# A two-layer generator backbone on one core: the framework's order of instructions made with a simulated time line

## The chip, the core and the metric

The kernel runs on one NeuronCore of a Trainium2 chip. Five engines work side by side, each through its own queue in order: TensorE (PE, matmuls and transposes, results in PSUM), VectorE (DVE), ScalarE (ACT), GpSimd (POOL) and SyncE (SP, which here issues DMAs). An instruction that needs another engine's result waits for a semaphore, and everything behind it in its queue waits too. The metric is the device time of one execution in microseconds, as the median of several runs.

## The reference

Two layers over 256 latent tokens, with 256 context tokens beside them in layer 0, model width 1024. Each layer is a token mixer and then a convolutional feed-forward network (FFN 2816 wide); each of the two is followed by a LayerNorm of a weighted sum. Layer 0 mixes by a bidirectional mLSTM (4 heads, inner width 2048), layer 1 by multi-head latent attention (8 heads). Shift, scale and gate of each sub-layer come from the condition vectors.

```python
ml = _modulation(c, ada_w[i], ada_b[i])            # six vectors: shift, scale, gate, twice
hl = _modulate(x, ml[0], ml[1])
yl, yc = mixer(hl, hc, ...)                        # mLSTM in layer 0, MLA in layer 1
x = _layer_norm(ALPHA * x + ml[2] * yl, ln_g[i, 0], ln_b[i, 0])
f = _conv_ffn(_modulate(x, ml[3], ml[4]), ffn_w_in[i], ffn_conv_w[i], ffn_conv_b[i], ffn_w_out[i])
x = _layer_norm(ALPHA * x + ml[5] * f, ln_g[i, 1], ln_b[i, 1])
```

In layer 0 the context goes through the same weights, with its own modulation. In layer 1 it only gives keys and values.

## The kernel before

**Products.** Every float32 product is three matmuls of split operands, in `mm3`: hi·hi (L383), hi·lo (L384) and lo·hi (L385), where hi is the operand rounded to TensorE's fast float32 form and lo is the rest. So every weight block of 128 x 1024 needs three steps before use: a DMA into `raw`, a cast on ScalarE (L323) that gives hi, and a subtraction on VectorE (L326) that gives lo. The class `Stream` does this in the order of use, up to eight blocks ahead (`AHEAD`), with three ordinary split buffers (`w`, `NB`) and some wide ones (`wu`). In the same way activations are split by `split` (L388 the cast, L389 the subtraction).

**Stages, in order of time.** `start_up` (first modulation and the first five `up` products), `w_up`, `w_og`, `w_v` (up to about 400 us), `w_qk` with the heads of the mLSTM, then the output product "mout", once for the context (`pc`) and once for the latent tokens (`pl`), the FFN of layer 0 (`ffn_pre`, `ffn_in`, then `w_fout0` with the products y21, y22 and yt4), the keys and values of layer 1 (`mla_ctx`, `mla_kv`, tiles dkv, kn and v), `mla`, the output product "aout", the FFN of layer 1 and its output product "fout1" with the last LayerNorm.

**Work beside the products.** Much of the VectorE and ScalarE work is in Python generators, which the product loops advance a step at a time (`tick`, `drain`): `head` (mLSTM weights W, lines 1008 to 1037: exponentials, multiplication with the scores, normalisation at L1023 and L1025, transposes PT at L1037), `post` (normalisation of a head's output `oh` at L1107, transposes `hnT` at L1113, result `hn`), `ln_rows` (gate L1141, residual L1142, statistics L1144, normalisation L1172 and L1173), `ln_T` (transposes `zT` at L1199, modulation `zm`, split into `h0`, `hc`, `hl` or `h1` at L1211 and L1212), `ln_x` (L1227, L1228), and in `w_fout0` the residual (gate L1441, addition L1442). A second list, `bg2`, spreads the modulation vectors of the later sub-layers over the products: one gate sum `junk` on VectorE (L512) per row block, let go by a small ScalarE copy (`gate`, L527).

**Product tails.** `outmm` multiplies one weight block with all banks of the output before the next block. For the last blocks (`TAIL`: 4 in mout, 7 in aout, 6 in fout1) it holds the weights and writes the loops the other way round, bank by bank, so that the first banks are finished early:

```python
            for t in range(2):
                for ps, cs in pss[t]:
                    for k, w in zip(tail, ws):
                        mms(k, w, t, ps, cs)
```

**What sets the order.** The program text is not the order of each engine's queue. The framework (`tile.TileContext`) tracks the dependencies between tiles, gives out buffers and semaphores, and lets its scheduler choose the order in which the instructions are put in the engines' queues. Two things bind it: `manual_schedule` around `start_up` keeps TensorE, VectorE and ScalarE in the written order there, and `keep_in_program_order` pins a few single instructions. Everything else is at the scheduler's choice.

## Time and profile before

| | |
|---|---|
| median of 3 runs | 1388.25 us (1387.74 to 1389.04) |
| profiled execution, its own time | 1389.13 us |
| its span in the profile | 1387.4 us, 19172 instructions |
| mean granted TensorE clock | 0.997 |
| TensorE matmuls busy | 1355.8 us (98 % of the span), 6903 |
| VectorE busy | 1075.0 us (77 %) |
| ScalarE busy | 699.2 us (50 %) |
| GpSimd busy | 121.2 us (9 %) |
| HBM | 262.90 MB read, 33.46 MB written, 214 GB/s over the span |

A row of the profile's groups has the line of the kernel, the engine, the operation, `out<-in` by tile names, the count, then the busy time and the mean time of one in ns, then the idle time of the engine ahead of them with what ended it. In the timeline a row has start, duration, engine, line and operation, and in brackets the idle time before it and what it waited for. PEld is TensorE's loading of the stationary operand, which overlaps the matmuls.

### The profile page before, as it was taken

The numbers are of one execution on the slowest core, as the hardware profiler recorded it, in microseconds if no ns is written. First come the engines' busy times: TensorE is split into PE (matmuls) and PEld (weight loads), VectorE is DVE, ScalarE is ACT, GpSimd is POOL, SyncE is SP. The second block draws the span as 40 slices with busy tenths as digits, with TensorE's granted clock in tenths as the row PEclk, the third lists the DMA queues.
The fourth block names the chain that finished last, engine by engine and source line by source line (L and its number), as shares of the span: only waits on it lengthen the run. The fifth ranks groups of instructions, "written<-read, shape, count | busy, mean of one in ns | idle before, by whom it ended". The sixth has DMA issues, their size and how long they took to land.

```text
span 1387.4 us, 19172 instructions
## 1 busy us (share of the span) xinstructions
PE 1355.8 (98%) x6903; PEld 1140.1 (82%) x6903; DVE 1075.0 (77%) x1726; ACT 699.2 (50%) x1179; POOL 121.2 (9%) x215
## 2 busy tenths in 40 slices
PE   7999999999999999999999999999999999999997
PEld 3788888888788888878798888888777898899986
DVE  6599757687688697788799878668898789777773
ACT  6585534435444545375643434334547567455560
POOL 0033000011011011120002000000001001000000
PEclk9999999999999999999999999999999999999999
DMA  9689847879666374766747877647987426367750
GB/s 339 217 292 325 289 152 248 237 261 326 210 205 203 104 231 140 242 196 223 242 143 242 295 234 234 211 148 234 310 224 224 137 99 207 116 188 230 209 183 31
DMA packets 97903, 297.63 MB, mean 215 GB/s; under 512 B 12136, under 2 KB 24808, under 8 KB 97808
## 3 DMA queue, kind: packets, MB, share of 16 engines
q1 hardware_dynamic: 68672, 218.52, 48.9%
q0 software_dynamic: 17472, 57.57, 13.4%
q10 hardware_dynamic: 11664, 20.32, 4.0%
q8 instruction: 54, 0.88, 0.3%
q14 instruction: 41, 0.34, 0.1%
HBM read 262.90 MB, written 33.46 MB: 214 GB/s over the span
## 4 chain that ended last, share of the span: by engine, by line
PE 86%; DVE 7%; DMA 3%; ACT 2%; issue 2%; ACTq 0%; SPq 0%; DVEq 0%
PE fin L383 9%; PE fin L384 9%; PE fin L385 9%; PE tok L383 6%; PE tok L385 6%; PE tok L384 6%; PE qk L383 4%; PE qk L384 4%; PE qk L385 4%; PE y L384 4%; PE y L385 4%; PE y L383 4%; PE up L383 2%; PE up L385 2%; PE up L384 2%
## 5 line engine op out<-in xcount | busy, mean ns | idle before, releaser
L326 DVE TENSOR_TENSOR w<-raw,w 128x1024 fp32r<-128x1024 f32 (+3 forms) x290 | 347.9, 1203 | 159.1 <-ACT w L323 158.3
L323 ACT CAST w<-raw 128x1024 fp32r<-128x1024 f32 (+3 forms) x290 | 300.3, 1037 | 331.6 <-PE fin L385 105.0
L384 PE MATMUL fin<-h,w 128*128 128x256 f32 (+1 forms) x696 | 231.7, 333 | 0.0
L385 PE MATMUL fin<-h,w 128*128 128x256 f32 (+1 forms) x696 | 231.4, 333 | 0.0
L383 PE MATMUL fin<-h,w 128*128 128x256 f32 (+1 forms) x696 | 231.2, 333 | 0.1
L512 DVE SCALAR_TENSOR_TENSOR junk<-ar,bc 128x1024 f32<-128x1024 f32 x128 | 155.9, 1218 | 4.9 <-ACT bc L554 2.3
L384 PEld LDWEIGHTS fin<-h,w 128*128 128x128 f32 x696 | 132.2, 190 | 13.0 <-DVE h L1212 0.2
L383 PEld LDWEIGHTS fin<-h,w 128*128 128x128 f32 x696 | 131.9, 190 | 13.2 <-ACT h L1211 0.3
L385 PEld LDWEIGHTS fin<-h,w 128*128 128x128 f32 x696 | 132.2, 190 | 12.7
L383 PE MATMUL qk<-xc,w 128*128 128x512 f32 x256 | 100.7, 393 | 0.0
L385 PE MATMUL qk<-xc,w 128*128 128x512 f32 x256 | 99.9, 390 | 0.0
L384 PE MATMUL qk<-xc,w 128*128 128x512 f32 x256 | 99.8, 390 | 0.0
L383 PEld LDWEIGHTS qk<-xc,w 128*128 128x128 f32 x256 | 48.1, 188 | 10.2 <-issue 0.4
L385 PEld LDWEIGHTS qk<-xc,w 128*128 128x128 f32 x256 | 48.1, 188 | 9.9
L384 PEld LDWEIGHTS qk<-xc,w 128*128 128x128 f32 x256 | 48.1, 188 | 9.6
L383 PE MATMUL up<-hT,w 128*128 128x512 f32 x128 | 50.5, 394 | 0.5 <-ACT hT L388 0.5
L384 PE MATMUL up<-hT,w 128*128 128x512 f32 x128 | 50.1, 392 | 0.4 <-DVE hT L389 0.4
L385 PE MATMUL up<-hT,w 128*128 128x512 f32 x128 | 50.1, 391 | 0.3 <-DVE w L389 0.3
L383 PE MATMUL tok<-w,hT 128*128 128x512 f32 x128 | 49.8, 389 | 0.0
L384 PE MATMUL tok<-w,hT 128*128 128x512 f32 x128 | 49.8, 389 | 0.0
L385 PE MATMUL tok<-w,hT 128*128 128x512 f32 x128 | 49.8, 389 | 0.0
L326 DVE TENSOR_TENSOR wu<-raw,wu 128x1024 fp32r<-128x1024 f32 (+1 forms) x33 | 39.1, 1200 | 8.2 <-ACT wu L323 7.9
(453 smaller groups left out, 3036.6 us busy)
## 6 DMA issues: line engine op xcount, KB each, us to landing
raw<-in_ws SPq DMA_DIRECT2D x287, 512.0 KB, 4.5
ar<-in_adaT SPq DMA_DIRECT2D x80, 512.0 KB, 4.7
adaw<-in_ada_w SPq DMA_DIRECT2D x32, 256.0 KB, 6.5
t2d<-raw ACTq DMA_DIRECT2D x13, 512.0 KB, 6.2
raw<-t2d SPq DMA_DIRECT2D x13, 512.0 KB, 6.3
raw<-in_ws POOLq DMA_DIRECT2D x13, 512.0 KB, 8.0
zr<-fd ACTq DMA_DIRECT2D x33, 128.0 KB, 3.2
xmd<-xr POOLq DMA_DIRECT2D x16, 256.0 KB, 5.4
```

Source lines behind the costliest of these rows:

```text
L323: k.nc.scalar.copy(h[:, :cols], src)
L326: k.nc.vector.tensor_sub(l[:, :cols], src, h[:, :cols])
L383: mm(out, w[0], x[0], start=start, stop=False)
L384: mm(out, w[0], x[1], start=False, stop=False)
L385: mm(out, w[1], x[0], start=False, stop=stop)
L512: nc.vector.scalar_tensor_tensor(o, w, 1.0, self.bc[j], op0=ALU.mult, op1=ALU.mult, accum_out=col[:, k, j:j + 1])
```

## The change

The one statement in `kernel` that opens the framework's context, at L1967, is given an option. With it the scheduler chooses its order along a simulated time line of the engines, instead of by its default rule. Kernel functions, buffers, constants and pins stay as they are.

```diff
-    with tile.TileContext(nc) as tc:
+    with tile.TileContext(nc, schedule_with_timeline_sim=True) as tc:
         build(tc, off, aps, out)
```

## The prediction

> **What bounds the kernel now.** I read the busy shares first, then the chain of work that ended last.

> ```profile
> PE 1355.8 (98%) x6903; PEld 1140.1 (82%) x6903; DVE 1075.0 (77%) x1726; ACT 699.2 (50%) x1179; POOL 121.2 (9%) x215
> PE 86%; DVE 7%; DMA 3%; ACT 2%; issue 2%; ACTq 0%; SPq 0%; DVEq 0%
> ```

> TensorE is busy for 1355.8 of 1387.4 us. The change leaves every instruction in place and alters only the order, so TensorE's own work is the same. All that can be won is its idle time, 31.6 us, and all that can be lost is new idle time. The second view is the busy time by stretch (the columns are stretch, its length, then PE, PEld, DVE, ACT and POOL busy with their counts, TensorE's granted clock, DMA share, GB/s).

> ```profile
> 0.00:100.00 100.00, 89.86 (x378) 62.04 (x379) 71.29 (x106) 66.72 (x108) 11.35 (x25) 1.00 0.82 281
> 100.00:600.00 500.00, 499.97 (x2261) 411.09 (x2260) 375.96 (x603) 236.53 (x406) 53.83 (x94) 1.00 0.70 225
> 600.00:700.00 100.00, 98.05 (x462) 80.33 (x461) 86.14 (x147) 59.92 (x105) 8.70 (x16) 1.00 0.74 234
> 700.00:1000.00 300.00, 299.91 (x1397) 251.11 (x1396) 243.91 (x369) 125.98 (x203) 21.64 (x40) 1.00 0.69 225
> 1000.00:1100.00 100.00, 91.51 (x472) 77.28 (x470) 89.82 (x169) 58.80 (x113) 9.72 (x14) 0.98 0.71 216
> 1100.00:1200.00 100.00, 96.95 (x627) 87.02 (x628) 86.35 (x162) 63.74 (x121) 6.20 (x12) 1.00 0.41 138
> ```

> Ten of the idle microseconds lie before 100 us (mostly the first loads) and 7.5 after 1300 us (the last LayerNorm, behind TensorE's last matmul). Between 100 and 600 us and between 700 and 1000 us there is nothing to win. That leaves 1.95 + 8.49 + 3.05 = 13.5 us in three stretches, the ones where VectorE is busy for 86 to 90 %. There TensorE and VectorE are both nearly full, and what counts is the order in which VectorE serves TensorE. The waits of TensorE (total us, times, longest) say who is late:

> ```profile
> PE adar L474 <- ACT adas L388: 6.7, 1, 6.7
> PE y L384 <- DVE w L326: 3.2, 3, 1.3
> PE y L383 <- ACT u L1421: 2.0, 1, 2.0
> PE zT L1199 <- DVE z L1172: 1.8, 1, 1.8
> PE dkv L383 <- ACT hl L1211: 1.5, 1, 1.5
> ```

> The first is the start, whose order on TensorE, VectorE and ScalarE is fixed by hand in both kernels. The other four are single events in the three stretches.

> **What the change does, part by part.** The built orders can be compared without times. The multiset of instructions is the same on every engine. The fewest instructions that must move to turn one order into the other are 587 of 6905 on TensorE, 417 of 1568 on VectorE, 201 of 1224 on ScalarE, 17 on GpSimd and 21 on SyncE. Three patterns hold most of them. (1) Where a weight's low half is awaited, TensorE now runs the hi·hi products (L383) of all open banks first. (2) The closing products of `outmm` (`last=True`), before done bank by bank, are interleaved over the banks. (3) On VectorE the weight subtractions L326 and the gate sums `junk` L512 are pulled ahead of head, residual and LayerNorm work, or, between 1004 and 1030 us, residual work is pulled ahead of L326. The prices of these movable pieces:

> ```profile
> L326 DVE TENSOR_TENSOR w<-raw,w 128x1024 fp32r<-128x1024 f32 (+3 forms) x290 | 347.9, 1203 | 159.1 <-ACT w L323 158.3
> L323 ACT CAST w<-raw 128x1024 fp32r<-128x1024 f32 (+3 forms) x290 | 300.3, 1037 | 331.6 <-PE fin L385 105.0
> L512 DVE SCALAR_TENSOR_TENSOR junk<-ar,bc 128x1024 f32<-128x1024 f32 x128 | 155.9, 1218 | 4.9 <-ACT bc L554 2.3
> ```

> *Zone A, 605 to 630 us (head 3 beside mout).* In before, VectorE finishes the attention weights W and TensorE transposes them at once:

> ```profile
> 607.53 0.50 PE L384 MATMUL y<-w,hn 128*128 128x512 f32 x1 [1.06 <-DVE w L326]
> 610.79 0.74 DVE L1025 SCALAR_TENSOR_TENSOR W<-W,R 128x512 f32<-128x512 f32 x1
> 611.73 0.82 PE L1037 MATMUL PT<-ident,W 128*128 128x128 f32 x6
> 614.67 1.67 DVE L1107 TENSOR_SCALAR oh<-oh,ss 128x512 f32<-128x512 f32 x4
> 620.70 0.39 PE L385 MATMUL y<-w,hn 128*128 128x512 f32 x1
> ```

> In the new order that last W operation stands 15 places later. Counted from 605.1 us, VectorE must first do six L326 and five junk sums (starts 1.14 us apart: 12.5 us), the four oh (1.6) and some 4.3 us of small work: 18.4 us, so W ends at 623.5 without any wait, and at about 625.7 if two of the pulled-ahead subtractions wait a cast of 1037 ns each. TensorE's transposes were pushed 37 places back, which gives cover: it does the mout products up to those that ended at 620.7 in before. It gains the 1.06 us wait and a smaller one, and so gets there at about 619.7. It stalls 3.8 to 6 us, then the chain transposes, split, next products adds about 1.5 us. I take the longer stall, since raw weights arrive just in time here (DMA share 0.74 in this stretch), so net +7.5; bounds +2.6 to +8.5.

> *Zone B, 690 to 708 us (mout tail, LayerNorm, ffn_pre).*

> ```profile
> 694.81 0.68 DVE L1141 TENSOR_TENSOR z<-y,gate 128x512 f32<-128x512 f32 x1
> 706.79 0.54 DVE L1172 TENSOR_SCALAR z<-z,mv,rs 128x512 f32<-128x512 f32 x1
> 707.90 1.80 PE L1199 MATMUL zT<-ident,z 128*128 128x128 f32 x15
> ```

> Before, the first bank is finished 8 us ahead of the last, and VectorE's twelve LayerNorm operations start at 694.8, beside the other banks. In the new order all four banks end within 1.6 us of the tail's end, and a junk sum stands ahead of the first L1141. VectorE then begins at 698.5, has 12 operations of 0.6 us and the small ones, and reaches the last L1172 at about 707.3 to 708.0. TensorE's cover (ffn_pre up to 707.9) is used up to the last 0.6 us already, so nearly all of that delay is paid: +1, bounds -0.8 (only the covered wait at 690.5) to +4.

> *Zone C, 1004 to 1085 us (FFN products y21, y22, yt4 and the key/value part of layer 1).*

> ```profile
> 1004.00 0.50 PE L383 MATMUL y<-w,fz 128*128 128x512 f32 x1 [2.04 <-ACT u L1421]
> 1020.52 1.21 DVE L326 TENSOR_TENSOR w<-raw,w 128x1024 fp32r<-128x1024 f32 x1
> 1023.26 0.39 PE L384 MATMUL y<-w,fz 128*128 128x512 f32 x1
> 1027.72 0.50 PE L384 MATMUL y<-w,fz 128*128 128x512 f32 x1 [1.35 <-DVE w L326]
> ```

> The residual operations L1441 and L1442 (0.6 us each) now stand ahead of the subtractions. The subtraction that ends at 1021.7 in before stands ten places later: from 1003.5 us VectorE has 5 full subtractions ahead of and with it and some 30 shorter operations, which ends at about 1027.5. TensorE wants that half at 1023.3, so it stalls there. After it the next one (1027.7 in before) is no longer the late one, so the net delay by 1030 us is 3 us, not 4.3. Later in the zone z_norm and the hc and hl copies stand 3 to 8 places back, behind weight subtractions and behind L1227/L1228; TensorE waits there already (1.5 us for hl), so such delays are paid in full: another +3, since several come in a row and part of each is hidden by the one before. Zone C +6, bounds +1 to +9.

> *Zone E, 1174 to 1192 us (aout tail, LayerNorm, first FFN products of layer 1).*

> ```profile
> 1174.00 0.39 PE L385 MATMUL y<-wu,oT 128*128 128x512 f32 x1
> 1175.54 0.68 DVE L1141 TENSOR_TENSOR z<-y,gate 128x512 f32<-128x512 f32 x1
> 1186.39 0.28 PE L385 MATMUL y<-wu,oT 128*128 128x256 f32 x1
> 1188.96 0.54 DVE L1172 TENSOR_SCALAR z<-z,mv,rs 128x512 f32<-128x512 f32 x1
> 1189.56 1.53 PE L1199 MATMUL zT<-ident,z 128*128 128x128 f32 x12 [1.84 <-DVE z L1172]
> ```

> Before, the first bank ends at 1174.0, 12.4 us ahead of the last, and only a bank of 256 columns is left for VectorE after 1186.4; the normalisation follows 2.6 us later. Interleaved, the first two banks end about 5.2 us ahead of the last. VectorE then has two L326 and the operations of all five banks to do, some 10.5 us of work from 1181.2 on, so the normalisation comes about 6 us after the last matmul. TensorE has nothing else to do there: +3.5, bounds +1.5 to +4.5.

> *The rest.* A head's normalisation at 1155 us stands behind one more subtraction: +0.5 (0 to +1). The low-half waits left over, 3.2 us less those already counted, and small ones go to pattern (1): -1 (-3 to 0). Between 100 and 600, 700 and 1000, and after 1200 us the swaps cost nothing, because TensorE is full and its operands are ready some microseconds ahead; if that cover failed, one swap costs one L326, 1.2 us. The 21 moved DMA issues on SyncE and the 17 on GpSimd shift by a few places in queues; I price them at nothing, bounded by one weight load's turn, 1.2 us of subtraction, per zone.

> *The clock.* These stretches show the granted clock as the first column after POOL:

> ```profile
> 1078.00:1081.00 3.00, 1.49 (x10) 1.04 (x8) 3.00 (x7) 2.42 (x7) 0.00 (x0) 1.00 0.00 0
> 1081.00:1084.00 3.00, 2.90 (x14) 2.77 (x14) 3.00 (x9) 2.36 (x7) 0.00 (x0) 0.70 0.00 0
> 1084.00:1087.00 3.00, 3.00 (x18) 3.00 (x17) 3.00 (x6) 0.83 (x1) 1.09 (x2) 0.73 0.10 38
> ...
> 1004.00:1007.00 3.00, 3.00 (x12) 2.29 (x13) 2.96 (x6) 1.39 (x2) 0.00 (x0) 1.00 1.04 401
> 1190.00:1193.00 3.00, 2.58 (x22) 2.34 (x21) 2.26 (x7) 2.86 (x8) 0.00 (x0) 1.00 0.00 0
> ```

> After the stall at 1080 us the clock fell to 0.70 and 0.73 for two stretches: 3 x 0.30 + 3 x 0.27 = 1.7 us of matmul time lost. After the stalls of 2.04 us (at 1004) and 1.84 us (at 1189.6) it stayed at 1.00. I count one more such dip, behind the long stall of zone A: +1.7, bounds 0 to +5 (three dips). [...]

> **Sum.** 7.5 + 1 + 6 + 3.5 + 0.5 - 1 + 1.7 = +19.2 us. The profiled execution took 1389.13 us (span 1387.4), 0.9 above the median of the three runs, 1388.25. So 1408.3 against its own time, and 1407.5 as a median.

> **Rivals.** *The order is better (faster).* The scheduler's time line may have the durations right, and then pattern (1) covers the low-half waits and the pulled-ahead work of VectorE arrives in time. It is decided at the zone A transposes and the mout and aout tails: if TensorE does not wait there more than before, what is left is the gain, 3.2 + 2.0 us of waits and parts of the others, at most 13.5: about -4 to -9 us, 1379 to 1384. For it: TensorE's moves do cover the right waits. Against: VectorE's totals per zone, which no order can shrink, and the banks that end late. 0.13.

> *Only the tails hurt.* W and the residuals come in time because VectorE's waits for casts shrink, and only B, E and some of C are paid: +5 to +9 us, 1393 to 1397. 0.17. *Much slower.* The stalls set VectorE and the loads behind, the delays of zone C add instead of hiding each other, and each long stall brings its dip (three of 1.7): 9 + 8.5 + 4 + 4.5 + 5 + 1 = +32 us, 1420. 0.12. *No change.* That the switch does nothing is excluded by the 587 moved matmuls; that gains and losses cancel within 0.2 % (2.8 us, about what a measurement of this kernel tells from no change) I give 0.04.

> **The numbers.** The forecast, +10 to +26 us, has 0.54. The forecast with the two slower rivals makes slower 0.83, faster 0.13, same 0.04. The range from 1391 to 1424 takes in the tails-only case and half of the much slower one.

> **What would show it.** Right: a PE wait of 3 us or more for W (PT transposes) near 620 us; a stall of several us at zT after the aout tail, near 1190; a wait at the y products for L326 at about 1018 to 1028; 600 to 700 us with 6 to 9 us more idle; a clock below 1.00 just after. The low-half wait at 607.5 should be gone. Wrong: if the stretch 600 to 700 us has no more idle time than 2 us, my reading of VectorE's queue fails; if the loss sits in 100 to 600 or 700 to 1000 us, the cover that I relied on is not there.

## The result, and the profile after

The changed kernel takes 1429.12 us (median of 4 runs, 1427.27 to 1429.33), the kernel before, on the same chip, 1387.99 us (4 runs). The ratio is 1.0288, with a 95 % interval of 1.0275 to 1.0301: 41 us slower. The profiled execution took 1427.27 us (span 1425.5), the fastest of the four, 38.1 us above that of before.

The page of the changed kernel, busy shares and the chain of work that ended last:

```profile
PE 1364.2 (96%) x6903; PEld 1147.2 (80%) x6903; DVE 1072.0 (75%) x1726; ACT 697.0 (49%) x1179; POOL 121.9 (9%) x215
PE 48%; DVE 4%; ACT 2%; issue 1%; DMA 1%; DVEq 0%; ACTq 0%
```

VectorE and ScalarE do the same work in the same busy time, to 0.3 %. TensorE does the same 6903 matmuls, but they now count 8.4 us more (1364.2 - 1355.8), for the most part the clock by the estimate further down, and its idle time grew from 31.6 to 61.3 us. The waits of TensorE (total us, times, longest) in the changed kernel, the largest but for those of the start:

```profile
PE PT L1037 <- DVE W L1025: 8.7, 2, 5.5
PE zT L1199 <- ACT z L1170: 6.0, 1, 6.0
PE y L384 <- DVE w L326: 4.7, 4, 1.8
PE zT L1199 <- DVE rs L1149: 3.8, 1, 3.8
PE hnT L1113 <- DVE oh L1107: 2.5, 1, 2.5
PE o L383 <- ACT PT L388: 2.4, 3, 1.2
PE dkv L383 <- ACT hc L1211: 2.3, 2, 1.3
PE kn L383 <- ACT wu L323: 2.2, 2, 1.5
PE dkv L383 <- ACT hl L1211: 1.7, 1, 1.7
PE kn L383 <- DVE kn L389: 1.3, 1, 1.3
```

None of the first, second, fourth and fifth stands in the list of before. They are the waits for W (5.5 us in zone A, the other 3.2 us near 443 us), for the LayerNorm behind the aout tail (E, where the wait before was 1.8 us), for the one behind the mout tail (B) and for oh (A again). The waits for low halves, which the new order of TensorE seems made to cover, have grown from 3.2 to 4.7 us.

Where the time went can be read to some 0.4 us, since both kernels have the same number of matmuls: the start of the n-th matmul in one trace less that in the other is the delay at that point (where the orders differ, the n-th need not be the same matmul). By stages (times are those of the kernel before), the delay added in the profiled execution of each kernel, in us:

| stage | 0 to 435 | 435 to 601 | A, 601 to 669 | B, 669 to 721 | 721 to 998 | C, 998 to 1082 | 1082 to 1173 | E, 1173 to 1193 | end | sum |
|---|---|---|---|---|---|---|---|---|---|---|
| changed kernel | -0.2 | +2.8 | +11.9 | +4.9 | 0 | +10.0 | +3.5 | +4.8 | 0 | +37.6 |
| forecast, of its sum | 0 | 0 | +7.5, +1.7 clock | +1 | 0 | +6 | +0.5 | +3.5 | 0 | +19.2, with -1 for small waits in no one stage |

### The profile page after: what moved, and what is told of

The parts are those of the page before. It is cut to its first block, busy times and chain, and to the rows that moved or that the text cites. A ratio compares the mean times of both kernels' runs of the same rounds, so it can differ in the third digit from the quotient of the medians.

```text
span 1425.5 us, 19179 instructions
## 1 busy us (share of the span) xinstructions
PE 1364.2 (96%) x6903; PEld 1147.2 (80%) x6903; DVE 1072.0 (75%) x1726; ACT 697.0 (49%) x1179; POOL 121.9 (9%) x215
## 4 chain that ended last, share of the span: by engine, by line
PE 48%; DVE 4%; ACT 2%; issue 1%; DMA 1%; DVEq 0%; ACTq 0%
PE fin L383 8%; PE fin L384 8%; PE fin L385 8%; PE y L384 5%; PE y L383 5%; PE y L385 5%; DMA raw<-in_ws 1%; PE zT L1199 1%; DVE w L326 1%; ACT zm L1206 1%; DVE z L1142 0%; PE PT L1741 0%; DVE st L1144 0%; PE dkv L385 0%; PE s L1722 0%
## 5 line engine op out<-in xcount | busy, mean ns | idle before, releaser
L323 ACT CAST w<-raw 128x1024 fp32r<-128x1024 f32 (+3 forms) x290 | 300.5, 1037 | 395.3 <-PE fin L385 139.6
L326 DVE TENSOR_TENSOR w<-raw,w 128x1024 fp32r<-128x1024 f32 (+3 forms) x290 | 348.6, 1203 | 185.5 <-ACT w L323 183.0
L383 PE MATMUL fin<-h,w 128*128 128x256 f32 (+1 forms) x696 | 231.6, 334 | 0.3 <-ACT w L323 0.2
L384 PE MATMUL fin<-h,w 128*128 128x256 f32 (+1 forms) x696 | 231.7, 333 | 0.0
L385 PE MATMUL fin<-h,w 128*128 128x256 f32 (+1 forms) x696 | 231.2, 333 | 0.0
L512 DVE SCALAR_TENSOR_TENSOR junk<-ar,bc 128x1024 f32<-128x1024 f32 x128 | 155.9, 1218 | 0.7
L383 PEld LDWEIGHTS fin<-h,w 128*128 128x128 f32 x696 | 132.1, 191 | 14.0 <-ACT w L323 1.0
L384 PEld LDWEIGHTS fin<-h,w 128*128 128x128 f32 x696 | 132.2, 190 | 13.1 <-DVE h L1212 0.2
L385 PEld LDWEIGHTS fin<-h,w 128*128 128x128 f32 x696 | 132.2, 190 | 12.7
L383 PE MATMUL qk<-xc,w 128*128 128x512 f32 x256 | 100.6, 393 | 0.0
L385 PE MATMUL qk<-xc,w 128*128 128x512 f32 x256 | 99.9, 390 | 0.0
L384 PE MATMUL qk<-xc,w 128*128 128x512 f32 x256 | 99.8, 390 | 0.0
L383 PEld LDWEIGHTS qk<-xc,w 128*128 128x128 f32 x256 | 48.1, 188 | 10.2 <-issue 0.4
L385 PEld LDWEIGHTS qk<-xc,w 128*128 128x128 f32 x256 | 48.1, 188 | 10.0
L384 PEld LDWEIGHTS qk<-xc,w 128*128 128x128 f32 x256 | 48.1, 188 | 9.8
L383 PE MATMUL up<-hT,w 128*128 128x512 f32 x128 | 50.5, 394 | 0.5 <-ACT hT L388 0.5
L384 PE MATMUL up<-hT,w 128*128 128x512 f32 x128 | 50.1, 392 | 0.5 <-DVE hT L389 0.5
L385 PE MATMUL up<-hT,w 128*128 128x512 f32 x128 | 50.1, 391 | 0.3 <-DVE w L389 0.3
L383 PE MATMUL tok<-w,hT 128*128 128x512 f32 x128 | 49.8, 389 | 0.0
L384 PE MATMUL tok<-w,hT 128*128 128x512 f32 x128 | 49.8, 389 | 0.0
L385 PE MATMUL tok<-w,hT 128*128 128x512 f32 x128 | 49.8, 389 | 0.0
L326 DVE TENSOR_TENSOR wu<-raw,wu 128x1024 fp32r<-128x1024 f32 (+1 forms) x33 | 38.9, 1201 | 7.4 <-ACT wu L323 7.2
```

Of the source, the lines that this page charges most:

```text
L323: k.nc.scalar.copy(h[:, :cols], src)
L326: k.nc.vector.tensor_sub(l[:, :cols], src, h[:, :cols])
L383: mm(out, w[0], x[0], start=start, stop=False)
L384: mm(out, w[0], x[1], start=False, stop=False)
L385: mm(out, w[1], x[0], start=False, stop=stop)
L512: nc.vector.scalar_tensor_tensor(o, w, 1.0, self.bc[j], op0=ALU.mult, op1=ALU.mult, accum_out=col[:, k, j:j + 1])
```

## The experiments

All kernels were built so that the order of a queue can be given: `pin` adds, between neighbours of a list, an edge that only orders them on their engine and waits for nothing.

```python
def pin(tc, *orders):
    ins = {i.name: i for i in tc.nc.cur_bb.bb.instructions}
    info = mybir.DependencyInfo(mybir.DependencyClass.NoSync, mybir.DependencyReason.DATA)
    for o in orders:
        ...
        for p, c in zip(ns, ns[1:]):
            tc.add_manual_dep(ins["I-%d" % c], "I-%d" % p, info, reason="pin")
```

### Whose order is it? One engine's queue at a time

My theory V put the loss on VectorE's order; the rivals were TensorE's order (T) and casts or loads (D). Four kernels pin one queue each.

```diff
+        pin(tc, DVE_ORDER)    # e1: default scheduler, VectorE as in the changed kernel
+        pin(tc, PE_ORDER)     # e2: default scheduler, TensorE as in the changed kernel
+        pin(tc, DVE_ORDER)    # e3: the option, VectorE as in the kernel before
+        pin(tc, PE_ORDER)     # e4: the option, TensorE as in the kernel before
```

> Default scheduler, with VectorE's queue alone pinned by order edges (no waits) to the order that the changed kernel has; the other engines are ordered by the default rule around it (258 TensorE instructions move against the kernel before, 587 in the changed one). Theory V (VectorE's order is most of the loss: the head weights W near 615 us, the weight subtractions near 1020 us, the LayerNorm after the aout tail): +22 to +32 us, with a wait for W of over 3 us. Rival T (TensorE's order is the loss: transposes pushed back, product tails interleaved so that no bank ends early): at most +8 us. Rival D (casts on ScalarE or the loads' order): at most +8 us.

> Default scheduler, with TensorE's queue alone pinned to the order of the changed kernel; VectorE then differs from the kernel before in 177 instructions instead of 417. Theory V: +6 to +14 us, from the interleaved tails of mout and aout only, and no wait for W of over 2 us. Rival T: +30 us or more. Rival D: +6 us at most.

> The changed kernel's scheduler option, with VectorE's queue alone pinned to the order of the kernel before. TensorE is ordered by the time line around it (604 instructions moved against the kernel before). Theory V: +5 to +14 us over the kernel before, with the loss near 1020 us and at W gone. Rival T: +25 us or more. Rival D: +25 us or more.

> The changed kernel's scheduler option, with TensorE's queue alone pinned to the order of the kernel before; VectorE has 372 instructions moved against the kernel before. Theory V: +20 to +32 us. Rival T: at most +8 us. Rival D: +25 us or more.

Measured, against 1387.88 us for the kernel before: e1 1445.66 us (ratio 1.0419, 1.0401 to 1.0436), e2 1416.27 (1.0203, 1.0188 to 1.0219), e3 1430.51 (1.0309, 1.0293 to 1.0324), e4 1424.59 (1.0265, 1.0250 to 1.0280). By stages:

| stage | 435 to 601 | A | B | C | 1082 to 1173 | E | sum |
|---|---|---|---|---|---|---|---|
| changed kernel | +2.8 | +11.9 | +4.9 | +10.0 | +3.5 | +4.8 | +37.6 |
| e1, VectorE new | +6.6 | +17.5 | +5.9 | +14.3 | +3.4 | +4.4 | +52.6 |
| e2, TensorE new | -0.6 | +9.5 | +3.7 | +6.4 | +2.1 | +5.6 | +27.1 |
| e3, VectorE old | -0.5 | +7.4 | +4.8 | +12.3 | +11.8 | +7.2 | +42.3 |
| e4, TensorE old | +2.0 | +16.7 | -0.1 | +10.4 | +5.9 | +0.9 | +35.7 |

No theory passes: every kernel lies above what V allowed it, and T and D fail as well, each on at least two. VectorE's new order alone costs more than all new orders together, and giving VectorE its old order back returns nothing. TensorE's new order alone (e2) costs less than all together. I read this so: the orders of the queues fit one another, and one queue taken from either order forces the others to wait in its sequence. These four runs do not show it by themselves, because the scheduler also sorts the other queues anew around the pinned one. Two stages do speak. The loss at 443 us, a wait for W which I had not foreseen, is there with VectorE's new order (e1, the changed kernel) and not with its old one or with TensorE's new one (e3, e2). In B and E, TensorE's old order (e4) leaves +0.8 of 9.7 us, but the stages ahead of them pay 4.8 and 2.4 us more.

### Is the loss made within each zone?

Here all five queues are pinned, to one kernel's order outside a zone and to the other's inside it, so that the orders stay fitted.

```diff
+        pin(tc, PE_ORDER, DVE_ORDER, ACT_ORDER, SP_ORDER, POOL_ORDER)
```

> The changed kernel with all five queues pinned to its own orders, except that the instructions of zone A (590 to 655 us of the kernel before: head 3 beside mout) and of zone E (1163 to 1200 us: aout tail and its LayerNorm) stand in the order of the kernel before, on every engine. Theory S (the loss is made zone by zone, in the order within each zone, and the zones add): zone A cost 11.6 us and E some 5 us in the trace of the changed kernel, so 1429 - 17 = 1412 us (1409 to 1416). Rival G (a delay in one zone buys slack that the next zone uses, so that an undone zone only moves its loss on): over 1420 us.

> The opposite splice: all five queues in the order of the kernel before, except zones A and E, which stand in the order of the changed kernel. Theory S: 1388 + 17 = 1405 us (1401 to 1408), with the waits for W (over 4 us) and zT after the aout tail. Rival G: at most 1396 us or over 1415 us.

> The order of the kernel before, except zone B (655 to 730 us: mout tail and the LayerNorm after it) and zone C (995 to 1090 us: y21, y22, yt4 and the keys and values of layer 1) in the order of the changed kernel. Theory S: B 5 us and C 10 us, 1388 + 15 = 1403 us (1399 to 1406). Rival G: at most 1396 us or over 1412 us.

Measured, against 1388.81 us: e5 1420.11 us (1.0233, 1.0216 to 1.0250), e6 1404.07 (1.0109, 1.0094 to 1.0124), e7 1405.48 (1.0124, 1.0109 to 1.0139). The waits of e6, the order of before with only A and E new:

```profile
PE zT L1199 <- ACT z L1170: 6.0, 1, 6.0
PE PT L1037 <- DVE W L1025: 5.8, 1, 5.8
PE hnT L1113 <- DVE oh L1107: 2.6, 1, 2.6
```

They are the waits of the changed kernel in these zones, to 0.3 us. By stages e6 adds 10.8 us in A and 4.6 in E (the changed kernel 11.9 and 4.8), e7 adds 4.3 in B and 11.3 in C (4.9 and 10.0), and neither adds more than 1.1 us anywhere else. (Behind C, e6 is 1.5 us faster than before.) So the order within the zones is slow by itself, and theory S holds for e6 and e7. It fails for e5: 1420.11 us lies outside its 1409 to 1416 and at the bound of theory G, over 1420. Zone A up to 635 us is as in before and E costs 0.8 us, but the stretch from 635 to 669 us, where the orders meet, loses 4.0 us to low halves, and the stages 435 to 601 and C cost about 1.5 us each more than in the changed kernel. So the zones do not add exactly: 8 us less came back than theory S had, and how much of that is the seam between the two orders stays open.

### Zone A: one wait behind another

In the changed kernel the timeline of VectorE (start, duration, operation) shows W's last step behind the pulled-ahead work, and that of TensorE who waits for it:

```profile
622.72 1.22 DVE L326 TENSOR_TENSOR w<-raw,w 128x1024 fp32r<-128x1024 f32 x1
623.86 0.69 DVE L389 TENSOR_TENSOR v<-vr,v 128x512 fp32r<-128x512 f32 x1
624.46 1.22 DVE L326 TENSOR_TENSOR w<-raw,w 128x1024 fp32r<-128x1024 f32 x1
625.60 1.22 DVE L512 SCALAR_TENSOR_TENSOR junk<-ar,bc 128x1024 f32<-128x1024 f32 x1
...
627.14 1.22 DVE L512 SCALAR_TENSOR_TENSOR junk<-ar,bc 128x1024 f32<-128x1024 f32 x1
...
628.28 0.75 DVE L1025 SCALAR_TENSOR_TENSOR W<-W,R 128x512 f32<-128x512 f32 x1
```

```profile
621.68 1.90 PE L1113 MATMUL hnT<-ident,oh 128*128 128x128 f32 x8 [2.47 <-DVE oh L1107]
629.09 1.54 PE L1037 MATMUL PT<-ident,W 128*128 128x128 f32 x6 [5.51 <-DVE W L1025]
631.39 1.97 PE L1113 MATMUL hnT<-ident,oh 128*128 128x128 f32 x8 [0.76 <-DVE PT L389]
```

The first experiment moves W's last four VectorE instructions up, the second moves five gate sums down, the third does both. Everything else is pinned as in the changed kernel.

```diff
 DVE_ORDER: ... 5097 (first R operation)
+5098 5099 5100 5101 (R, R, L1023, L1025)                    e9, e12
 ...
-5209 ... 5263 ... 5305 ... 5415 ... 5453 (five junk, L512)   e11, e12
 ... 5260 (last hn operation)
+5209 5263 5305 5415 5453                                     e11, e12
```

> The changed kernel with all queues pinned to its own orders and four VectorE instructions moved: the last steps of the head weights W of head 3 (two small R operations, L1023 and L1025) stand right behind the first R operation, instead of 25 places later. If W's place in VectorE's queue is the wait of 5.5 us at the PT transposes, TensorE no longer waits there, and 4 to 7 us come back: 1422 to 1425 us. If TensorE would only wait for the next thing (oh, hnT, a weight half): at most 2 us come back, 1427 us or more.

> The changed kernel with all queues pinned to its own orders, except that five gate sums (junk, L512, 1.14 us each, fill work that nothing waits for here) stand behind the hn operations of head 2 instead of ahead of W, oh and the PT splits. Theory Q (TensorE's waits in zone A, for oh, for W and for the bank that the PT split frees, are the length of VectorE's queue ahead of each): the bank is freed 4.6 us earlier and zone A costs 5 to 7 us instead of 11.6, 1422 to 1425 us. Rival (the late thing is not the queue but the inputs, casts and loads): at most 2 us come back, 1427 us or more.

> The changed kernel with all queues pinned to its own orders, with both moves on VectorE in zone A: the last steps of W right behind the first R operation, and the five gate sums behind the hn operations. If each wait of zone A is only the length of VectorE's queue ahead of what TensorE needs (oh, W, then the bank that the PT split frees), the two moves add: 11.6 us of zone A fall to 4 to 6, 1421 to 1424 us, and no wait for W is left. If the moves cover the same time (the bank is freed by an operation behind both), no more than the better of the two alone: 1425 us or more.

Measured: e9 1426.37 us (ratio to before 1.0276, 1.0260 to 1.0291), e11 1425.42 (1.0269, 1.0255 to 1.0284), e12 1420.41 (1.0220, 1.0204 to 1.0235). In the stage table A costs 9.1, 8.7 and 3.0 us. In e9 TensorE no longer waits for W, yet little comes back:

```profile
623.22 1.63 PE L1113 MATMUL hnT<-ident,oh 128*128 128x128 f32 x8 [1.49 <-DVE oh L1107]
624.69 0.82 PE L1037 MATMUL PT<-ident,W 128*128 128x128 f32 x6
630.35 1.97 PE L1113 MATMUL hnT<-ident,oh 128*128 128x128 f32 x8 [4.85 <-DVE PT L389]
```

The transposes PT now run at 624.7, 4.4 us earlier, and the next transposes wait 4.85 us instead. They need the PSUM bank that PT filled, and that bank is freed by VectorE's split of PT (L389), which stands behind the same subtractions and gate sums. So the wait moved to the next thing, as the rival said, although the time, 2.8 us below the changed kernel, lies between the two forecasts. With the gate sums moved as well (e12) these transposes run at 626.2:

```profile
622.79 0.82 PE L1037 MATMUL PT<-ident,W 128*128 128x128 f32 x6
626.24 1.25 PE L1113 MATMUL hnT<-ident,oh 128*128 128x128 f32 x8 [2.62 <-DVE PT L389]
```

The two moves alone return 2.8 and 3.2 us of zone A, together 8.9 of 11.9. So e11 returned less than it was forecast to (8.7 us of zone A left, not 5 to 7), and e12 more (3.0 left, not 4 to 6). This shows the mechanism of the zone: W, oh and the bank are served by one in-order queue, and moving nine instructions gives back three quarters of it. That both moves return more than the sum of each, 6.0 us, is in part the clock: between 604 and 690 us the mean granted clock is 0.92 in the changed kernel and 1.00 in e12, where the dip that begins at 622.4 us is gone.

### The product tails

> The changed kernel's scheduler option, with the matmuls of the product tails (outmm, last=True) chained bank by bank as the program writes them; nothing else is pinned, the other engines are ordered by the time line around it. Theory T for zones B and E (the loss there is made by TensorE's interleaved tails, which leave all LayerNorm work of VectorE behind the last matmul): zone E gives back 4 to 5 us and zone B 4 to 6, 1418 to 1422 us. Rival (VectorE's own order makes it, its LayerNorm operations stand behind subtractions in any case): at most 3 us come back, 1426 us or more.

```diff
+            done = []
             for t in range(2):
                 for ps, cs in pss[t]:
                     for k, w in zip(tail, ws):
-                        mms(k, w, t, ps, cs)
+                        done += mms(k, w, t, ps, cs)
+            for p, c in zip(done, done[1:]):
+                self.tc.add_manual_dep(c.ins, p.ins.name, mybir.DependencyInfo(
+                    mybir.DependencyClass.NoSync, mybir.DependencyReason.DATA), reason="bank by bank")
```

Measured: 1428.21 us (1.0291, 1.0277 to 1.0305), nothing back. The wait behind the aout tail fell from 6.0 to 2.45 us, but the tails themselves now wait:

```profile
705.54 0.51 PE L383 MATMUL y<-wu,hn 128*128 128x512 f32 x1 [2.78 <-ACT wu L323]
706.80 0.50 PE L384 MATMUL y<-wu,hn 128*128 128x512 f32 x1 [0.76 <-DVE wu L326]
...
1225.28 1.71 PE L1199 MATMUL zT<-ident,z 128*128 128x128 f32 x12 [2.45 <-DVE z L1172]
```

Bank by bank, the first bank needs all held weights at once, and the casts and subtractions come too late for that. B costs 5.8 us (4.9 in the changed kernel), and what E gives back (1.2 instead of 4.8) is paid in the stage ahead of it (6.1 instead of 3.5). So my theory for B and E, that TensorE's interleaving alone is the loss, falls. That the interleaved order suits weights that come late is my reading, and no run tests it.

### Can the gains be had alone?

The traces show three small gains: the 1.2 us between 443 and 601, where TensorE's transposes stand in one block; some 1.0 us at 1004 us; and covered low-half waits. Two kernels try for them.

```diff
+            mm(out, w[1], x[0], start=False, stop=False)
+            mm(out, w[0], x[1], start=False, stop=stop)     # e10: the weight's low half last
...
+        pin(tc, ...)    # e13: the order of before, but for 455 to 590 and 1000 to 1010 us
```

> The kernel before with the default scheduler, and one change in the program: where the streamed weight is the moving operand (outmm and the products of w_fout0), the three matmuls of a product run hi-hi, lo-hi, hi-lo, so that the weight's low half is asked for last. If the part of the changed order that is worth having is the cover of the low-half waits (5.0 us over zones A, B and C in the kernel before, of which each order covers a part): 1 to 3 us faster, 1385 to 1387 us. If VectorE is the bound there, TensorE only waits at the next weight: within 0.5 us of the kernel before.

> The kernel before with all five queues pinned to its order, except two stretches in the order of the changed kernel: 455 to 590 us, where transposes that stood in small groups between matmuls stand in one block (the trace of the changed kernel gains 1.2 us there), and 1000 to 1010 us, where it gains 1.0 us. If these gains are made within the stretch and nothing behind takes them back: 2.2 us faster, 1385.5 to 1386.5. If the next wait of VectorE-bound zones takes them back: within 0.8 us of the kernel before.

Measured: e10 1389.07 us against 1387.84 (ratio 1.0009, 1.0000 to 1.0018), e13 1389.13 us against 1389.53 (0.9998, 0.9989 to 1.0007). Neither is faster. In e10 the low-half wait fell from 3.2 us to

```profile
PE y L386 <- DVE w L326: 0.8, 2, 0.6
PE av L383 <- DVE hn L1121: 1.2, 1, 1.2
```

(line numbers are 4 higher from mm3 on), and other waits, such as the second row, took the place. In e13 the first stretch gained 0.6 us and zone C lost 2.0. No kernel here is faster than the one before.

## Why the prediction was wrong

The sign and most of the places were right: 600 to 700, 1000 to 1100 and 1173 to 1193 us lose, 100 to 435, 721 to 998 and after 1193 us do not, the wait for W is there with 5.5 us where I had worked out 3.8 to 6. But 2.8 us are lost between 435 and 601 us, inside the stretch that was to lose nothing; that was one of my signs of being wrong. The size was half of what was measured, +19.2 against +38 in the profiled executions, and 1429.1 us lies 5 us above the range. One reading was loose without harm: the wait for low halves in the trace of before is three events, not one. Term by term:

**Zone A, +7.5 and +1.7, measured 11.9.** The stall for W was sized right. The sum left out a stall of its own: 2.5 us for oh, which stands in the same queue. I had treated the wait for W as the one event of the zone; e9 and e12 show that three waits follow one another there. Its dip of the clock, by the estimate below half of 7.4 us, was also twice as large as priced.

**Zone B, +1, measured 4.9, over its upper bound.** I let VectorE begin the LayerNorm at 698.5, because I took the time of the subtraction ahead of it from the trace of before. In the changed kernel that subtraction waits for its cast, and the LayerNorm waits behind it although its banks are finished (VectorE's timeline; in brackets its idle time):

```profile
711.52 1.23 DVE L326 TENSOR_TENSOR w<-raw,w 128x1024 fp32r<-128x1024 f32 x1 [1.66 <-ACT w L323]
713.59 1.23 DVE L326 TENSOR_TENSOR w<-raw,w 128x1024 fp32r<-128x1024 f32 x1 [0.84 <-ACT w L323]
714.73 1.22 DVE L512 SCALAR_TENSOR_TENSOR junk<-ar,bc 128x1024 f32<-128x1024 f32 x1
715.87 2.48 DVE L1141 TENSOR_TENSOR z<-y,gate 128x512 f32<-128x512 f32 x4
724.61 0.54 DVE L1172 TENSOR_SCALAR z<-z,mv,rs 128x512 f32<-128x512 f32 x1
```

TensorE is 12.7 us late by then, so 715.87 answers to 703.2: the start is 4.7 us later than I had it. The chain after it is as worked out, 8.7 us to the last L1172. The chain that ended last (start, duration) shows where the 4.7 us come from:

```profile
698.98 1.23 DVE wu L326
700.22 5.50 DMA raw<-in_ws
705.74 1.06 ACT wu L323
...
708.08 4.33 DMA raw<-in_ws
712.51 1.06 ACT w L323
```

Here a load starts when VectorE's work frees a buffer (between 680 and 716 us the loads' queue waits 11.2 us in all for subtractions of wu), and the next subtraction waits for that load and its cast. The cast at 712.51 answers to 699.8; in the trace of before it ran at 695.04, 4.8 us earlier. The failed step is that I kept the loads at their old times: a subtraction that stands ahead of the LayerNorm brings its own wait for a load with it, and passes it to everything behind. This is read from the traces; no run moves these subtractions alone.

**Zone C, +6, measured 10.0.** The first half came as worked out, 2.7 us by 1034 against 3. The second half cost 7.3 instead of 3. TensorE's waits for hc and hl grew by 2.9 us (from 0.3 + 1.5 us to 2.3 + 1.7, and 0.7 for the low half of hl), about the 3 that I had priced; that several delays would hide one another is not where it failed. The sum left out waits beside them: 2.2 us for casts of the weights wu and 1.3 us for the split of kn, both new. Together that is 6.4 of the 7.3 us, as read from the traces.

**Zone E, +3.5, measured 4.8.** The wait at zT is 6.0 us (1.8 in before), as the 6 us between the last matmul and the normalisation said. A dip of the clock came on top (0.50 for 6.83 us).

**435 to 601 and 1082 to 1173, 0 and +0.5, measured +2.8 and +3.5.** Here the claim that TensorE's operands are ready some microseconds ahead failed. At 443 us the weights W of another head stand behind pulled-ahead work just as in zone A, and TensorE waits 3.18 us. At 1122 to 1173 us TensorE waits 2.4 us for the splits of PT on ScalarE (`PE o L383 <- ACT PT L388` above); no experiment bears on this stage.

**The clock, +1.7, in the traces some 7.8.** I counted one more dip than in before, which has one; there are four (in both traces the clock also falls after TensorE's last matmul, at 1382.6 us in before and 1421.1 in the changed kernel; that is not counted). The granted clock is the first column after POOL (the first two rows are of one dip, from 622.4 to 636.0 us):

```profile
625.00:628.00 3.00, 0.00 (x0) 0.00 (x0) 3.00 (x5) 0.00 (x0) 0.00 (x0) 0.50 0.89 210
631.00:634.00 3.00, 2.61 (x10) 2.44 (x11) 3.00 (x6) 3.00 (x6) 0.94 (x3) 0.50 0.30 97
726.00:729.00 3.00, 3.00 (x18) 2.91 (x18) 2.07 (x5) 2.69 (x7) 0.00 (x0) 0.63 0.00 0
1110.00:1113.00 3.00, 2.77 (x11) 2.78 (x12) 3.00 (x9) 1.73 (x5) 0.00 (x0) 0.58 0.35 134
1225.00:1228.00 3.00, 2.82 (x13) 2.82 (x14) 1.13 (x3) 2.96 (x7) 0.00 (x0) 0.50 0.00 0
```

Inside these four dips the granted clock is 0.50, and TensorE is busy for 7.4 + 3.4 + 3.4 + 4.8 = 19.0 us; in the one of before it is busy for 3.4 us. By half of that, the dips cost some 7.8 us of matmul time more; this is an estimate from these busy times, near the 8.4 us by which the matmuls' busy time grew. Behind each of the stalls of 3.8, 5.5 and 6.0 us the rows have 0.50 to 0.63. But not all four dips begin in or behind such a stall: in zone A the clock had fallen at 622.4 us, behind the 2.5 us for oh and ahead of the 5.5 us for W, and at 1110 us the longest wait just ahead of the dip is 1.7 us. My reading of the trace of before, one dip in three stalls, had put the number too low; the last section sets the dips beside TensorE's busy time ahead of them.

What the terms for A, B and C share is the way in which they were worked out: the new order of one queue was laid on the times that the other engines and the loads had before. Each stall was then the last one. In fact the engine that waits is itself late for the next exchange. The rival "much slower", +32 us, was nearest to this: stalls that set VectorE and the loads behind, and a dip behind each. It had 0.12. It too put only 1 us on all that lies outside the four zones, where 6.3 us were lost.

## What to carry to other kernels

Where two engines are both nearly full, a queue's order is priced along the whole ring of exchanges (operand, transpose, split, freed PSUM bank), not at the first wait: taking the first wait away gave back 2.8 of 11.9 us, taking away what all three stood behind gave 8.9. Work that nothing waits for should not stand ahead of work that TensorE waits for (five gate sums moved back returned 3.2 us), and work that itself waits for a load passes its wait on to what stands behind it (4.7 us in zone B). An order of several queues is one thing: VectorE's queue taken over alone was worse (+52.6 us) than all of them together (+37.6), TensorE's alone was not (+27.1).

## What the runs showed of the hardware that was not expected

The same stall in the same order is not always followed by a clock dip. In the changed kernel and in e9 TensorE waits 3.18 us for W near 443 us; behind it the clock stays full in one and is half in the other:

```profile
438.07:441.48 3.41, 2.01 (x11) 1.44 (x10) 3.16 (x11) 1.71 (x4) 0.00 (x0) 1.00 0.90 290
441.48:444.90 3.42, 1.65 (x8) 1.44 (x9) 3.42 (x7) 0.00 (x0) 0.55 (x1) 1.00 0.55 165
444.90:448.30 3.40, 3.40 (x16) 2.80 (x15) 1.56 (x3) 0.00 (x0) 0.00 (x0) 1.00 0.66 224
```

```profile
439.76:443.17 3.41, 0.23 (x3) 0.13 (x2) 3.15 (x8) 1.44 (x4) 0.00 (x0) 1.00 0.53 177
443.17:446.58 3.41, 3.41 (x10) 2.73 (x11) 3.10 (x6) 0.00 (x0) 0.55 (x1) 0.50 0.66 193
```

The first rows are the changed kernel's, the second e9's. The dip costs 1.5 us (the stage 435 to 601 adds 2.8 us without and 4.3 with it, in e5, e9, e11 and e12), about the spread between the profiled execution of the changed kernel, 1427.27 us, and its other runs, 1429.03 to 1429.33 (mean granted clock 0.989, and 0.985 to 0.988 in the others). The clock records of the kernel before and of the changed one lie on a grid: every dip but the one that the end of each trace cuts off lasts 3.41 us or a whole multiple of it (13.65, 3.41, 3.41 and 6.83 us in the changed kernel, 3.41 in before), and begins a whole multiple of 3.41 us after the one before it (30, 113, 33 and 58 times in the changed kernel, 88 in before). Counted from the start of the span the grid lies at 1.2 us in the changed kernel, 0.2 in before and, by the rows above, 2.9 in e9. Those rows are cut along it. In e9 the stall falls into one piece of 3.41 us, in which TensorE is busy for 0.23 us; in the changed kernel it is shared by two, with 2.01 and 1.65 us.
